# Gate and up products in two halves, with their low sums in banks of the other group

## The chip, the cores and the metric

The kernel runs on one core of a Trainium2 chip. The metric is the time of one execution in device microseconds; before the change the median of 3 runs is 1695.89 us (1694.25 to 1705.35).

## The reference

Two request groups, 256 prompt frames and 64 new frames of a running stream, go through one layer with shared weights. Together they are T = 320 columns of D = 2048 features. The part that the change touches is the feed-forward network behind the second norm:

```
hn = rmsnorm(h, norm_ffn[l])
gu = hn @ w_gate_up[l]                                   # 2048 -> 2 x 5632
h = h + (silu(gu[..., :D_FF]) * gu[..., D_FF:]) @ w_down[l]
```

Ahead of it stand the norm, the input projection, stick-breaking attention, the spatial gate, the two branch projections and w_out; behind it the last norm. All data is float32.

## The kernel before, in words

Features lie on the 128 partitions, the 320 columns along the free dimension. Every float32 product is made of three products of shorter floats: a weight chunk `raw` is loaded on SP's queue, ACT rounds it to `wh` (line 554 in the feed-forward part, line 70 elsewhere) and DVE takes the rest, `wl` or `low` (lines 555 and 71). Three `raw` buffers and four `wh` buffers stand in a ring: the load of a chunk waits until DVE has split the chunk three before it, and a cast to `wh` waits until PE is through with the chunk four before it.

The feed-forward part runs in three slices of 16, 16 and 12 blocks of 128 hidden features. A slice takes four blocks at a time, as a *gate quad* and then an *up quad* (`quad`), so 8, 8 and 6 quads, and then multiplies by w_down: first six blocks side by side in two passes over k, then one block after the other (lines 87 to 89).

One quad works on four blocks and all 16 row chunks of 128, which come as 8 loads of 512 KB. For each load PE runs 20 *wide* products (line 562; two row chunks times five column pieces, with a piece of the activations as the stationary operand and 512 weight columns moving), in three main banks: three `acc` banks for a gate quad, three of four `aux` banks for an up quad. They give the sum with frames on partitions. After all 8 loads the 64 *low* products follow (line 572): four sums of 16, one per block, in the banks `aux1`, `aux`, `aux1`, `aux`, that DVE copies to `total` (line 573). A quad's low products need the low parts of all 8 chunks, so these stay until the last of the four sums; there are nine buffers for them.

The main banks have to be turned: `quad_turn` has ACT copy the three banks into `flat`, once for each 16-bit half (line 587, three copies each), and issue a DMA transpose after each three (line 588). `quad_join` has DVE put the transposed halves back (line 594, two), and add them to `total` (lines 596, 597). Then a gate quad's total is scaled and goes through Silu (lines 601, 602); an up quad's is scaled, multiplied with the gate's and split into `act` (lines 606 to 611).

Each engine runs its instructions in a fixed order, which a planner makes from the order in the code. Work that is late by intent is put off by ticks: `at(now + 5, ...)` calls a function when five ticks have gone by; a tick ends with each loaded chunk and, before the change, with each low sum.

In the w_out loop ahead of it, POOL's queue loads the residual input x in tiles `xr` (line 524), the first two as soon as the norm's result is there.

Of the kernel before, what the change touches and what calls it, by code (L numbers as in the profile page):

```python
# [34 lines left out]
def stream_step(ctx: ExitStack, tc: tile.TileContext, xT, w_in, w_a, w_b, w_out, w_gu, w_down,  # L35
# [484 lines left out]
    for m in range(KD):  # L520
        x = t320("xr")
# [18 lines left out]
    count = [0]  # L540

    def quad(b0, main, done):
        lows = []
        for c in range(0, KD, 2):
            raw = wraw.tile([P, HALF * P], F32, tag="raw", name="raw")
            nc.sync.dma_start(out=raw.rearrange("p (b k) -> p b k", b=4),
                              in_=w_gu[b0 : b0 + 4, :, c * P : (c + 2) * P].rearrange("b p k -> p b k"))
            wh = wsplit.tile([P, HALF * P], F32R, tag="wh", name="wh")
            if count[0] % 9 < 4:
                wl = wsplit.tile([P, HALF * P], F32R, tag="wl", name="wl")  # L550
            else:
                wl = fpool.tile([P, HALF * P], F32R, tag="low", bufs=5, name="low")
            count[0] += 1
            nc.scalar.copy(out=wh, in_=raw)  # L554
            nc.vector.tensor_tensor(out=wl, in0=raw, in1=wh.bitcast(F32), op=ALU.subtract)  # L555
            wh = wh.rearrange("p (b k) -> p b k", b=4)
            lows.append(wl)
            for j in range(2):
                k = c + j
                w, x = wh[:, :, j * P : (j + 1) * P], hg[k][2]  # L560
                for i, at0 in enumerate((0, T + TS, P, T + TS + P, TP)):
                    nc.tensor.matmul(main[i // 2].rearrange("p (b m) -> p b m", b=4), x[:, at0 : at0 + P], w,  # L562
                                     start=k == 0 and i % 2 == 0, stop=k == KD - 1 and (i % 2 == 1 or i == 4))
            tick()
        total = fpool.tile([P, 4, T], F32, tag="sum", bufs=2, name="sum")
        now = state["tick"]
        turning = quad_turn(main)
        for b in range(4):
            ps = aux1() if b % 2 == 0 else aux()
            for k in range(KD):  # L570
                at0 = (2 * b + k % 2) * P
                nc.tensor.matmul(ps[:, :T], lows[k // 2][:, at0 : at0 + P], hg[k][0], start=k == 0, stop=k == KD - 1)  # L572
            nc.vector.tensor_copy(total[:, b, :], ps[:, :T])  # L573
            tick()
# [16 lines left out]
    def quad_join(total, flat, turned):  # L591
# [12 lines left out]
    def up_out(gate, total, b):  # L604
# [3 lines left out]
        for j in range(2):  # L608
            a = pair("act", dt=F32R)
            nc.scalar.copy(out=a[:, 0, :], in_=t[:, j, :])  # L610
            nc.vector.tensor_tensor(out=a[:, 1, :], in0=t[:, j, :], in1=a[:, 0, :].bitcast(F32), op=ALU.subtract)
            act.append(a)
# [57 lines left out]
    def down_out(m, ps):  # L670
        nc.vector.tensor_tensor(out=hs[m], in0=ps[:, :T], in1=hs[m], op=ALU.add)
        if s0 + n < KF:
            return
# [6 lines left out]

    for s0, n in SLICES:
        act = []
        for b0 in range(s0, s0 + n, 4):
            gate = quad(b0, [acc() for _ in range(3)], gate_out)
            quad(KF + b0, [aux() for _ in range(3)], lambda total, b, gate=gate: up_out(gate, total, b))
        final = s0 + n == KF
        lead = [acc() for _ in range(3)] + [aux() for _ in range(3)]
        for k0, k1 in ((0, HALF), (HALF, n)):
            for m, ps in enumerate(lead):
# [3 lines left out]
                if k1 == n:  # L693
                    down_out(m, ps)
                tick()
        halves = [(t[:, 0, :], t[:, 1, :]) for t in act]
        for m in range(len(lead), KD - LATE if final else KD):
            down_out(m, block(w_down[m][:, s0 * P : (s0 + n) * P], halves))
# [147 lines left out]
```

## Time and profile before

| | us |
|---|---|
| median of 3 runs | 1695.89 (1694.25 to 1705.35) |
| the profiled execution | 1698.68 |
| its span | 1696.9 |
| PE busy | 1682.7 |
| DVE busy | 971.8 |
| ACT busy | 734.1 |

PE is the engine that multiplies; PEld are its weight loads, which overlap the products. Busy times of PE are modelled, so the pace of PE is read from when its instructions start, not from how long one lasts. The granted clock is 0.998 of full speed over the whole span. The span is what lies between the first and the last instruction, and the execution takes 1.8 us more.

### The profile page before, as it was taken

What the parts mean: (1) busy time and instruction counts of PE and PEld (TensorE: products, weight loads), DVE (VectorE), ACT (ScalarE), POOL (GpSimd) and SP (SyncE); (2) the same over time, 40 slices, a digit from 0 to 9 for tenths busy, and PEclk for the clock granted to TensorE, in tenths of its full rate; (3) what the DMA queues carried; (4) which work ended last, traced back from release to release, by engine and by line L of the source; (5) the groups of instructions that cost most, each with busy time, mean ns of one, the idle gap of its engine ahead of it and who ended that gap; (6) DMA issues with size and microseconds to landing.
All of it is one profiled execution on the core that took longest, in us unless ns stands there. A gap on an engine that the chain in (4) does not pass through costs nothing.

```text
span 1696.9 us, 25604 instructions
## 1 busy us (share of the span) xinstructions
PE 1682.7 (99%) x10496; PEld 1607.0 (95%) x10496; DVE 971.8 (57%) x1261; ACT 734.1 (43%) x956; POOL 38.9 (2%) x68
## 2 busy tenths in 40 slices
PE   9999999999999999999999999999999999999998
PEld 9999999999999999998988899988888999889898
DVE  7665656544444445556666664446666644475666
ACT  7555645433333333444444532343445323444343
POOL 1100001000000000000000000000000000000000
PEclk9999999999999999999999999999999999999999
DMA  7866555444444444556656655566666545566554
GB/s 280 258 178 177 160 163 164 118 152 151 151 149 149 150 149 162 173 167 178 175 173 182 193 167 150 156 166 170 180 167 189 166 150 162 164 189 174 149 156 124
DMA packets 236982, 285.49 MB, mean 168 GB/s; under 512 B 98081, under 2 KB 194337, under 8 KB 236865
## 3 DMA queue, kind: packets, MB, share of 16 engines
q1 hardware_dynamic: 164016, 257.72, 48.6%
q10 hardware_dynamic: 70224, 17.88, 6.0%
q0 software_dynamic: 2624, 8.26, 1.6%
q8 instruction: 82, 1.34, 0.3%
q14 instruction: 36, 0.29, 0.1%
HBM read 256.03 MB, written 5.51 MB: 154 GB/s over the span
## 4 chain that ended last, share of the span: by engine, by line
PE 87%; DMA 5%; DVE 4%; ACT 2%; issue 1%; ACTq 0%; SPq 0%; DVEq 0%
PE acc L89 18%; PE acc L87 18%; PE acc L88 18%; PE acc L562 9%; PE aux L572 8%; PE aux L562 7%; DMA raw<-w_gu 2%; DMA turned<-flat 2%; PE aux L89 2%; PE aux L88 2%; PE aux L87 2%; ACT flat L587 1%; DVE low L555 1%; DVE flat L594 1%; PE acc L639 1%
## 5 line engine op out<-in xcount | busy, mean ns | idle before, releaser
L70 ACT CAST wh<-raw 128x1024 fp32r<-128x1024 f32 (+2 forms) x296 | 302.7, 1023 | 561.1 <-PE acc L88 382.4
L71 DVE TENSOR_TENSOR wl<-raw,wh 128x1024 fp32r<-128x1024 f32 (+2 forms) x296 | 351.7, 1191 | 224.4 <-ACT wh L70 223.3
L87 PE MATMUL acc<-A,wh 128*128 128x320 f32 x1088 | 337.7, 311 | 0.4 <-ACT A L108 0.4
L88 PE MATMUL acc<-A,wh 128*128 128x320 f32 x1088 | 336.5, 309 | 0.0
L89 PE MATMUL acc<-A,wl 128*128 128x320 f32 x1088 | 336.3, 309 | 0.0
L554 ACT CAST wh<-raw 128x1024 fp32r<-128x1024 f32 x176 | 185.3, 1054 | 317.8 <-DMA raw<-w_gu 259.9
L87 PEld LDWEIGHTS acc<-A,wh 128*128 128x128 f32 x1088 | 204.4, 188 | 2.3 <-issue 1.5
L88 PEld LDWEIGHTS acc<-A,wh 128*128 128x128 f32 x1088 | 204.5, 188 | 0.3 <-DVE A L110 0.3
L89 PEld LDWEIGHTS acc<-A,wl 128*128 128x128 f32 x1088 | 204.3, 188 | 0.2 <-DVE wl L71 0.2
L562 PE MATMUL acc<-wh,A 128*128 128x512 f32 x880 | 203.2, 390 | 1.1 <-ACT wh L554 1.0
L562 PE MATMUL aux<-wh,A 128*128 128x512 f32 x880 | 201.5, 389 | 0.0
L562 PEld LDWEIGHTS acc<-wh,A 128*128 128x128 f32 x880 | 164.2, 188 | 37.0 <-ACT wh L554 3.5
L562 PEld LDWEIGHTS aux<-wh,A 128*128 128x128 f32 x880 | 164.8, 188 | 33.7
L89 PE MATMUL acc<-act,wl 128*128 128x320 f32 x500 | 155.1, 311 | 2.8 <-DVE wl L71 2.8
L87 PE MATMUL acc<-act,wh 128*128 128x320 f32 x500 | 155.0, 310 | 0.0
L88 PE MATMUL acc<-act,wh 128*128 128x320 f32 x500 | 154.9, 310 | 0.0
L555 DVE TENSOR_TENSOR low<-raw,wh 128x1024 fp32r<-128x1024 f32 x96 | 117.8, 1235 | 37.4 <-ACT wh L554 37.1
L573 DVE COPY sum<-aux 128x320 f32<-128x320 f32 x88 | 43.0, 489 | 157.8 <-PE aux L572 157.8
L572 PE MATMUL aux<-A,low 128*128 128x320 f32 x768 | 128.6, 309 | 0.1
L572 PEld LDWEIGHTS aux<-A,low 128*128 128x128 f32 x768 | 117.1, 188 | 1.4 <-ACT flat L587 0.4
L555 DVE TENSOR_TENSOR wl<-raw,wh 128x1024 fp32r<-128x1024 f32 x80 | 97.6, 1224 | 22.1 <-ACT wh L554 22.1
L572 PE MATMUL aux<-A,wl 128*128 128x320 f32 x640 | 109.0, 309 | 0.8 <-ACT flat L587 0.8
(221 smaller groups left out, 2297.5 us busy)
## 6 DMA issues: line engine op xcount, KB each, us to landing
raw<-w_gu SPq DMA_DIRECT2D x176, 512.0 KB, 3.8
raw<-w_in SPq DMA_DIRECT2D x141, 512.0 KB, 3.7
raw<-w_down SPq DMA_DIRECT2D x80, 512.0 KB, 3.7
raw<-w_out SPq DMA_DIRECT2D x32, 512.0 KB, 3.6
raw<-w_a SPq DMA_DIRECT2D x16, 512.0 KB, 3.4
raw<-w_b SPq DMA_DIRECT2D x16, 512.0 KB, 3.5
raw<-w_down SPq DMA_DIRECT2D x16, 256.0 KB, 2.8
xr<-xT POOLq DMA_DIRECT2D x16, 160.0 KB, 2.6
```

The lines of the kernel that those rows point to most:

```text
L70: nc.scalar.copy(out=wh[:, : n * P], in_=raw[:, : n * P])
L71: nc.vector.tensor_tensor(out=wl[:, : n * P], in0=raw[:, : n * P], in1=wh[:, : n * P].bitcast(F32), op=ALU.subtract)
L87: nc.tensor.matmul(ps[:, :T], a, x[0], start=first, stop=False)
L88: nc.tensor.matmul(ps[:, :T], a, x[1], start=False, stop=False)
L89: nc.tensor.matmul(ps[:, :T], b, x[0], start=False, stop=last)
L554: nc.scalar.copy(out=wh, in_=raw)
L555: nc.vector.tensor_tensor(out=wl, in0=raw, in1=wh.bitcast(F32), op=ALU.subtract)
L562: nc.tensor.matmul(main[i // 2].rearrange("p (b m) -> p b m", b=4), x[:, at0 : at0 + P], w, start=k == 0 and i % 2 == 0, stop=k == KD - 1 ...
L572: nc.tensor.matmul(ps[:, :T], lows[k // 2][:, at0 : at0 + P], hg[k][0], start=k == 0, stop=k == KD - 1)
L573: nc.vector.tensor_copy(total[:, b, :], ps[:, :T])
L587: tc.keep_in_program_order(nc.scalar.copy(out=planes[:, i, c * 512 : (c + 1) * 512], in_=hw[:, :, 1 - i]))
L594: nc.vector.tensor_copy(rows[:, :, :, :, 1 - i], turned[:, i].rearrange("p (c b) t -> p b c t", c=3))
```

## The change

`quad` goes through the row chunks in two halves: 4 loads with 40 wide products, then four low sums over these 4 chunks, then the same again. The wide products stay in the three main banks for both halves. The first half's low sums are copied to `total`, those of the second half are added to it. They take banks of either group: `BESIDE` lists them for a gate quad (turn 0) and an up quad (turn 1), half by half. The low parts have two sets of four buffers in turn. `total` has three buffers in place of two, and `quad_join` stands behind the last add in the planner's order. The put-off work counts from the end of the low sums: the join comes 3 ticks later, the output work 4 and 5; two low sums make one tick. The loads of x use the tag `ev`, which the gates use before them. `up_out` and `down_out` get arguments that leave their work as it is in the calls made here; `add_down` and the tag of `gate_quad` are not used.

```diff
-        x = t320("xr")
+        x = t320("ev")
...
+    LOWS = 4
+    MAIN = (acc, aux)
+    BESIDE = (((aux,) * 4, (aux, aux, aux1, aux)), ((acc, acc, acc, aux1), (acc, acc, aux, aux1)))
+
+    def quad(src, xs, done, tag="sum"):
...
+        main = [MAIN[turn_no]() for _ in range(3)]
+        total = fpool.tile([P, 4, T], F32, tag=tag, bufs=3 if tag == "sum" else 1, name=tag)
+        for half, c0 in enumerate((0, nk // 2)):
+            lows = []
+            for c in range(c0, c0 + nk // 2, 2):
...
+                if count[0] % (4 + LOWS) < 4:
+                    wl = wsplit.tile([P, HALF * P], F32R, tag="wl", name="wl")
+                else:
+                    wl = fpool.tile([P, HALF * P], F32R, tag="low", bufs=LOWS, name="low")
...
+            if half:
+                turning = quad_turn(main)
+            for b in range(4):
+                ps = BESIDE[turn_no][half][b]()
+                for k in range(nk // 2):
...
+                if half:
+                    last = nc.vector.tensor_tensor(out=total[:, b, :], in0=ps[:, :T], in1=total[:, b, :], op=ALU.add)
+                else:
+                    nc.vector.tensor_copy(total[:, b, :], ps[:, :T])
+                if b % 2:
+                    tick()
         now = state["tick"]
-        turning = quad_turn(main)
-        for b in range(4):
-            ps = aux1() if b % 2 == 0 else aux()
...
-        at(now + 5, quad_join, total, *turning)
+        at(now + 3, quad_join, last.ins, total, *turning)
         for i in range(2):
-            at(now + 6 + i, done, total, 2 * i)
+            at(now + 4 + i, done, total, 2 * i)
...
-    def quad_join(total, flat, turned):
+    def quad_join(behind, total, flat, turned):
+        with tc.issue_after(behind):
+            join(total, flat, turned)
```

How this moves instructions is seen at three places. The names are those of the tiles, `aux` with a number is the single bank `aux1`, and xN is a run of N alike. The first is PE's order over one gate quad. Before, in slice one:

```order
L562 MATMUL acc<-wh,A 128x512 x80
L572 MATMUL aux_7831<-A,wl 128x320 x8
L572 MATMUL aux_7831<-A,low 128x320 x8
L572 MATMUL aux<-A,wl 128x320 x8
L572 MATMUL aux<-A,low 128x320 x8
L572 MATMUL aux_7867<-A,wl 128x320 x8
L572 MATMUL aux_7867<-A,low 128x320 x8
L572 MATMUL aux<-A,wl 128x320 x8
L572 MATMUL aux<-A,low 128x320 x8
```

With the change, a gate quad (`acc`) and the first half of the up quad behind it (`aux`):

```order
L571 MATMUL acc<-wh,A 128x512 x40
L580 MATMUL aux<-A,wl 128x320 x32
L571 MATMUL acc<-wh,A 128x512 x40
L580 MATMUL aux<-A,low 128x320 x16
L580 MATMUL aux_8363<-A,low 128x320 x8
L580 MATMUL aux<-A,low 128x320 x8
L571 MATMUL aux<-wh,A 128x512 x40
L580 MATMUL acc<-A,wl 128x320 x24
```

The 80 wide products in a row are now 40 and 40, and half of the low products stand between them. A sum is 8 products long in place of 16, and the up quad's sums lie in `acc`.

The second place is DVE's order from the join of an up quad through the gate quad behind it. Before (an up quad's join, and the splits of the next gate quad):

```order
L594 COPY flat<-turned 128x1536
L573 COPY sum<-aux 128x320
L594 COPY flat<-turned 128x1536
L555 TENSOR_TENSOR low<-raw,wh 128x1024
L596 TENSOR_TENSOR sum<-flat,sum 128x1280
L555 TENSOR_TENSOR low<-raw,wh 128x1024
L597 TENSOR_TENSOR sum<-flat,sum 128x4x64
L555 TENSOR_TENSOR wl<-raw,wh 128x1024
L606 TENSOR_TENSOR sum<-sum,rh 128x640 x2
L607 TENSOR_TENSOR sum<-sum 128x640 x2
L555 TENSOR_TENSOR wl<-raw,wh 128x1024
L611 TENSOR_TENSOR act<-sum,act 128x320 x4
```

With the change, from the join to the last split of the gate quad's second half:

```order
L612 COPY flat<-turned 128x1536 x2
L564 TENSOR_TENSOR low<-raw,wh 128x1024
L614 TENSOR_TENSOR sum<-flat,sum 128x1280
L564 TENSOR_TENSOR low<-raw,wh 128x1024
L615 TENSOR_TENSOR sum<-flat,sum 128x4x64
L564 TENSOR_TENSOR low<-raw,wh 128x1024
L624 TENSOR_TENSOR sum<-sum,rh 128x640
L585 COPY sum<-aux 128x320
L625 TENSOR_TENSOR sum<-sum 128x640
L585 COPY sum<-aux 128x320
L624 TENSOR_TENSOR sum<-sum,rh 128x640
L631 TENSOR_TENSOR act<-sum,act 128x320 x2
```

and what follows these at once:

```order
L625 TENSOR_TENSOR sum<-sum 128x640
L585 COPY sum<-aux 128x320 x2
L631 TENSOR_TENSOR act<-sum,act 128x320 x2
L564 TENSOR_TENSOR low<-raw,wh 128x1024
L564 TENSOR_TENSOR wl<-raw,wh 128x1024 x3
L583 TENSOR_TENSOR sum<-aux,sum 128x320
L564 TENSOR_TENSOR wl<-raw,wh 128x1024
L583 TENSOR_TENSOR sum<-aux,sum 128x320
L583 TENSOR_TENSOR sum<-aux_9307,sum 128x320
L583 TENSOR_TENSOR sum<-aux,sum 128x320
```

The join of line 612 (594 before) waits for both transposes and stands behind all four sums of its quad, where it stood ahead of the last one. The splits of lines 564 that follow it are those of the second half of the quad that PE is in, the three of the row `x3` and the one behind the next add belong to the first half of the quad after that. The adds of line 583 are mixed with these.

The third place is ACT's order round the turn of that same gate quad with the change:

```order
L628 CAST act<-sum 128x320 x4
L563 CAST wh<-raw 128x1024 x3
L601 COPY flat<-acc 128x512 x3
L563 CAST wh<-raw 128x1024
L602 DMA_TRANSPOSE turned<-flat 128x12x128
L601 COPY flat<-acc 128x512 x3
L602 DMA_TRANSPOSE turned<-flat 128x12x128
L563 CAST wh<-raw 128x1024 x4
```

The casts `x3` ahead of the copies of line 601 are the first three chunks of the next quad. The copies stood behind three such casts before, too.

## Rows read from the trace of the kernel before

**Rows 1.** The page: span; busy time, share and count of each engine.
```profile
span 1696.9 us, 25604 instructions
...
PE 1682.7 (99%) x10496; PEld 1607.0 (95%) x10496; DVE 971.8 (57%) x1261; ACT 734.1 (43%) x956; POOL 38.9 (2%) x68
```

**Rows 2.** Stretches: length, busy of PE, PEld, DVE, ACT, POOL; clock; DMA.
```profile
760.88:981.19 220.31, 220.31 (x1154) 195.19 (x1153) 137.05 (x162) 105.27 (x138) 2.15 (x1) 1.00 0.65 179
1093.84:1318.34 224.50, 222.49 (x1154) 194.71 (x1153) 133.74 (x155) 101.78 (x133) 0.00 (x0) 1.00 0.64 174
1431.65:1596.90 165.25, 165.25 (x866) 146.41 (x865) 95.06 (x111) 75.00 (x98) 0.00 (x0) 1.00 0.62 175
1600.40:1603.70 3.30, 3.30 (x14) 3.30 (x15) 3.30 (x4) 0.00 (x0) 0.00 (x0) 0.56 0.61 169
```

**Rows 3.** Chain of waits, one quad: start, length, work.
```profile
871.20 18.16 PE acc L562 x80
889.36 9.38 PE aux L572 x64
```

**Rows 4.** Timeline of PE at the last slice's down blocks.
```profile
1596.90 0.31 PE L87 MATMUL acc<-act,wh 128*128 128x320 f32 x1
...
1600.33 0.64 PE L89 MATMUL acc<-act,wl 128*128 128x320 f32 x1 [2.39 <-DVE wl L71]
...
1603.38 0.30 PE L88 MATMUL acc<-act,wh 128*128 128x320 f32 x1
```

**Rows 5.** Waits of PE: us in total, times, longest.
```profile
PE acc L89 <- DVE wl L71: 2.8, 2, 2.4
```

**Rows 6.** Timeline of all engines in slice two, round a stall.
```profile
1208.43 1.07 DVE L594 COPY flat<-turned 128x1536 uint16<-128x1536 uint16 x1 [4.58 <-DMA turned<-flat]
...
1210.70 1.22 DVE L555 TENSOR_TENSOR low<-raw,wh 128x1024 fp32r<-128x1024 f32 x1
...
1215.45 1.05 ACT L554 CAST wh<-raw 128x1024 fp32r<-128x1024 f32 x1 [5.59 <-DMA raw<-w_gu]
...
1216.55 0.73 PE L562 MATMUL acc<-wh,A 128*128 128x512 f32 x2 [0.61 <-ACT wh L554]
```

**Rows 7.** Timeline of all engines, one quad's turn.
```profile
1227.35 1.55 ACT L587 COPY flat<-acc 128x512 uint16<-128x512 uint16 x3
...
1232.17 1.45 ACTq L588 DMA_TRANSPOSE turned<-flat  x1
...
1237.29 1.07 DVE L594 COPY flat<-turned 128x1536 uint16<-128x1536 uint16 x1 [2.56 <-DMA turned<-flat]
```

**Rows 8.** Transposes of the turned tile, all of them.
```profile
DMA to landing us min/median/max: 3.6/3.7/6.1
```

**Rows 9.** Groups: busy us, mean ns | idle, releaser.
```profile
L554 ACT CAST wh<-raw 128x1024 fp32r<-128x1024 f32 x176 | 185.3, 1054 | 317.8 <-DMA raw<-w_gu 259.9 <-PE acc L88 28.0 <-PE acc L562 22.5
...
L555 DVE TENSOR_TENSOR low<-raw,wh 128x1024 fp32r<-128x1024 f32 x96 | 117.8, 1235 | 37.4 <-ACT wh L554 37.1 <-PE aux L572 0.2
...
L594 DVE COPY flat<-turned 128x1536 uint16<-128x1536 uint16 x44 | 45.3, 1051 | 40.6 <-DMA turned<-flat 40.6
L573 DVE COPY sum<-aux 128x320 f32<-128x320 f32 x88 | 43.0, 489 | 157.8 <-PE aux L572 157.8
...
L596 DVE TENSOR_TENSOR sum<-flat,sum 128x1280 f32<-128x1280 f32 x22 | 32.8, 1492 | 0.0
...
L611 DVE TENSOR_TENSOR act<-sum,act 128x320 fp32r<-128x320 f32 x44 | 18.7, 491 | 0.1
...
L607 DVE TENSOR_TENSOR sum<-sum 128x640 f32<-128x640 f32 x22 | 17.1, 822 | 0.0
...
L671 DVE TENSOR_TENSOR h<-acc,h 128x320 f32<-128x320 f32 x33 | 16.2, 491 | 35.5 <-PE acc L89 35.5
...
L597 DVE TENSOR_TENSOR sum<-flat,sum 128x256 f32<-128x256 f32 x22 | 9.4, 426 | 0.0
```

**Rows 10.** Loads of line 524.
```profile
DMA to landing us min/median/max: 2.5/2.6/4.5
```

More of the change, by code (lines that the diff above doesn't have):

```diff
@@ L539, in stream_step @@
     fpool = fctx.enter_context(tc.tile_pool(name="ffn", bufs=1))
[L540 to L565, printed above, removed]
-        now = state["tick"]
-        turning = quad_turn(main)
-        for b in range(4):
-            ps = aux1() if b % 2 == 0 else aux()
[L570 to L574, printed above, removed]
-        at(now + 5, quad_join, total, *turning)
@@ L602, in gate_out, with up_out @@
         nc.scalar.activation(out=t, in_=t, func=AF.Silu)
-    def up_out(gate, total, b):
+    def up_out(to, apart, gate, total, b):
         t = total[:, b : b + 2, :]
@@ L610, in up_out, with add_down @@
             nc.scalar.copy(out=a[:, 0, :], in_=t[:, j, :])
-            nc.vector.tensor_tensor(out=a[:, 1, :], in0=t[:, j, :], in1=a[:, 0, :].bitcast(F32), op=ALU.subtract)
-            act.append(a)
+            flat = a.rearrange("p i t -> p (i t)")
+            for r0, r1, at0 in (((TP, T, T), (0, TP, T + TS)) if apart else ((0, T, T),)):
+                nc.vector.tensor_tensor(out=flat[:, at0 : at0 + r1 - r0], in0=t[:, j, r0:r1],
+                                        in1=a[:, 0, r0:r1].bitcast(F32), op=ALU.subtract)
+            to.append(a)
+    def add_down(m0, total, b):
+        y = ypair[(m0 + b) // 2]
+        nc.vector.tensor_tensor(out=y, in0=total[:, b : b + 2, :], in1=y, op=ALU.add)
     def gain(m, half):
@@ L668, in stream_step, with down_out @@
     LATE = 6
-    def down_out(m, ps):
+    def down_out(m, ps, final):
         nc.vector.tensor_tensor(out=hs[m], in0=ps[:, :T], in1=hs[m], op=ALU.add)
-        if s0 + n < KF:
+        if not final:
             return
@@ L679, in down_out, with gate_quad, up_quad @@
         nc.vector.tensor_scalar(out=hs[m], in0=hs[m], scalar1=g_fin[:, m : m + 1], scalar2=None, op0=ALU.mult)
+    wide_x = [t[2] for t in hg]
+    def gate_quad(b0, tag="sum"):
+        return quad(w_gu[b0 : b0 + 4], wide_x, gate_out, tag)
+    def up_quad(b0, gate, to, apart):
+        quad(w_gu[KF + b0 : KF + b0 + 4], wide_x, lambda total, b: up_out(to, apart, gate, total, b))
     for s0, n in SLICES:
@@ L683, in stream_step @@
         for b0 in range(s0, s0 + n, 4):
-            gate = quad(b0, [acc() for _ in range(3)], gate_out)
-            quad(KF + b0, [aux() for _ in range(3)], lambda total, b, gate=gate: up_out(gate, total, b))
+            up_quad(b0, gate_quad(b0), act, False)
         final = s0 + n == KF
```

28 lines of the change are left out of this document (26 added, 2 removed).

## The prediction

> **What bounds the kernel now.** I read the page first: PE is busy for 1682.7 of 1696.9 us, and no other engine for more than 58% [rows 1]. So all the time in which PE waits, from the first instruction to the last, is 14.2 us, 0.84% of the span. The change takes no product away (a quad keeps 80 wide and 64 low ones), so its gain has a ceiling below 1%.
>
> Next the chain of waits in an undisturbed stretch, for PE's pace: 80 wide products in 18.16 us (0.227 each), 64 low ones in 9.38 us (0.147 each), 27.54 us a quad [rows 3]. The last low product is followed by the next quad's first wide one with no gap; changing kind or bank costs nothing that the view shows.
>
> Then the stretches, one for the quads of each slice [rows 2]. The first has 8 quads in 220.31 us, which is 8 x 27.54; the third 6 in 165.25, which is 6 x 27.54. Only the second is longer: 224.50, so 4.19 us of stalls. Round one of them [rows 6] the reader sees how it comes about: DVE sits 4.58 us in the join at line 594 for a transpose, and the split of a chunk stands behind the join in its queue; that split ends at 1211.92, its raw buffer is loaded again and the cast begins at 1215.45, 3.53 us later; PE starts its wide products at 1216.55, having waited.
>
> The other place is the start of the down blocks. In the last slice 17 products start from 1596.90 up to 1603.38, 6.48 us where 17 x 0.147 are 2.49: 3.99 us lost, of which 2.39 are a wait for DVE's split [rows 4]. The rest is the clock: it is granted at 0.56 on average over the 3.3 us behind the wait [rows 2], so part of them ran at 1.2 GHz. The same wait in an earlier slice cost the other 0.4 of 2.8 us [rows 5].
>
> What the change can give back is therefore 4.19 + 3.99 + 0.4 = **8.6 us**.
>
> **The change, part by part.**
>
> *Halves.* No product more or less, and switches between wide and low cost nothing by rows 3. What changes is cover. Before, the nine buffers of low parts held a whole quad of eight chunks until its last low sum, so DVE could split only one chunk ahead. Now a half holds four of eight buffers, and DVE splits the next half's four while PE is in this one (the order shows the splits of the second half ahead of the copies of the first half's sums). A load has then 13.77 us of PE's time to come for every four chunks; one takes 3.53 from split to cast [rows 6]. The 4.19 us go. At the down blocks the first four splits now stand ahead of the join, so the 4.4 us there go too.
>
> *Sums.* 88 copies become 88 copies and 88 adds on DVE. The copy takes 0.489 us, an add out of PSUM into SBUF of the same size 0.491 (line 671) [rows 9]: 43 us more on an engine that is idle for 725. Beside PE's work this is nothing; what it does to DVE's queue is the next point.
>
> *DVE's queue behind the join.* This is the price. Put 0 at the end of an up quad's last wide product, with a gate quad next. ACT copies the main banks at once; from the first copy to the second transpose's issue it is 4.82 us [rows 7]; the transpose lands after 3.7 at the median [rows 8]. DVE joins from 8.5 on. Then, in the order of the new rows, and with the mean durations [rows 9]: two joins 2.1, a split 1.24, 1.49 for line 596, a split, 0.43 for line 597, a split: 16.3. Four scalings at 0.82, four subtractions for act at 0.49, four copies at 0.49 and the fourth split: 24.7. PE needs that split for its low sums at 27.54, so this is just in time.
>
> But the raw buffer of the third chunk of the next quad comes free only then. Its cast begins 3.53 later, at 28.3, and ends at 29.3 [rows 6, 9]. ACT's copies of the gate quad's main banks, ready at 27.54, stand behind that cast. The fourth cast follows the first three copies (1.55 us, [rows 7]) and ends at 31.9, its split at 33.2, and DVE's add of the second low sum, which stands behind the split, at 33.7. That sum lies in the third main bank of the up quad to come. PE has ended the gate quad's low products at 27.54 + 4.69 = 32.23, and reaches this bank with its fifth wide product, 0.91 later, at 33.1. **It waits 0.6 us.**
>
> There is one such place for each gate quad behind an up quad of its slice, and PE waits at the up quad that follows: 3 + 3 + 2 = 8 places, 4.6 us. Behind a gate quad's join DVE has 1.64 us to do in place of 5.2, and by the same count the fourth split ends 3.6 us earlier: no wait. Ends of the range: below, 0 a place, since instructions of DVE that follow each other overlap a little (the 44 of line 611 would be 21.6 us by their mean and are 18.7 [rows 9], 0.07 each), which over the 17 on this path is more than 0.6. Above, the longest landing, 6.1 us [rows 8], shifts everything by 2.4: 3.0 a place, 24 us. I take 0.6, with the median landing: the long ones come where several loads are issued next to the transpose, and here DVE has no more than one split to do between its adds and the join.
>
> *Join and output later.* The join is issued 2 chunks later and behind the last add. Its own transposes keep their place on ACT's queue. Who waits: the single `flat` tile, needed again 27 us on; and `act` at the slice's end, needed in the second pass of the down blocks, 21 us (six blocks of 24 products at 0.147) behind the last low sum. By the queue above it is ready some 20 us behind the last wide product, 15 behind the last low sum. Nothing.
>
> *x in `ev`.* POOL's loads of x wait for the last gates, no longer for the first norm; the two early ones move behind all other loads of POOL's queue. They land in 2.6 us, 4.5 at most [rows 10]; between the last gate and the first add of x lie the branch products and w_out's first block, 96 products of 0.147, 14 us. Nothing; without that cover 2.6 us once. The buffers for `total`, and the new arguments, issue no instruction.
>
> **The sum.** 1698.7 (the profiled execution) - 8.6 + 4.6 = 1694.7. That execution is 2.8 above the median of the runs, so **1692 us** against 1695.9, less than can be told from no change (about 1%, 17 us).
>
> **The rivals.**
>
> *The backlog of DVE's queue is deeper.* From 1.1 us a place on (8.6 / 8) the change gives back more than it takes, which is a join only 0.5 us later than I count. The trace has such joins: one began 5.1 us after the issue [rows 7], 1.4 later than the median landing, so 2.0 a place, 16 us, and 1703. With the longest landing 24 us: 1711. For it speaks that the wait closes on itself: late splits make late loads, these make late copies, these a late join. Against it that a gate quad's join is lighter and resets the queue. Slower by over 1% needs 3.2 us a place, more than the longest landing gives alone; a load that is late too could do it.
>
> *It doesn't do what it says.* Three slices with the same order have 0, 4.19 and 0 us of stalls in the quads, so these hang on when transposes land, and the join still stands ahead of a split. If the new cover does not reach, the stalls stay: 1696.
>
> *Half the clock.* PE's clock fell to its lower level behind a wait of 2.4 us [rows 2, 4]. If bank changes, now every 8 low products, left such holes, the low parts would run at that level: 11 products took 3.05 us there, 0.277 each [rows 4], so 64 x 22 x 0.13 = 183 us more, 1875. The trace speaks against it: banks change every 16 low products now, and the clock stays at 1.00 through all quads [rows 2]. By that row the low parts add 0. The Trainium skill has the rule that speaks for this rival (TensorE: Matmul & The Clock Gate, "A second HAM failure mode: psum-queue depth-cycling"): going through PSUM banks in each iteration can leave PE short idle times between its groups, frequent enough for the clock to swing between its levels and cost throughput. By it the sum would be 1875 in place of 1692.
>
> **How the numbers follow.** My forecast (waits under 1.1 us a place): 0.60, from 1687 to 1696. The backlog: 0.30, 1696 to 1711, of which 0.05 slower by over 1%. No effect: 0.07. The clock: 0.03. Slower by over 1% is then 0.08, faster by over 1% 0.01 (the ceiling forbids it; the rest is for what I have not seen), no change 0.91. The range for 8 in 10 runs from 1685 (all 8.6 back, and the runs' spread of 1.6 downward) to 1705 (2.0 us a place, and 1.6 upward); it leaves out the upper half of the backlog and the clock.
>
> **What would show it.** In the second slice eight quads in 220.3 us plus three waits; no wait of line 89 for a split at the last down blocks, and the clock at 1.00 there. Each up quad but a slice's first begins with four wide products and then a wait of about 0.6 us that DVE's add (line 583) ends. The first copy of line 601 comes 1 to 2 us behind the last wide product of these gate quads, at once in up quads. I am wrong if PE waits anywhere else in the quads, if these waits are over 1.1 us, or if the low products are further apart than 0.147 us.

## The result, and the profile after

Over 20 runs of each, the changed kernel takes **1706.55 us** at the median (1700.59 to 1711.09), the kernel before 1697.11 (1691.75 to 1708.54): ratio 1.0047, 95% interval 1.0032 to 1.0062. It is half a per cent slower, 9.4 us. The profiled executions are 12.4 us of span apart; the places below add up to that. The one of the changed kernel, at 1711.09, is the slowest of its 20, so it shows more waiting than a median run: 1706.55 is 16 us above the 1690.4 of runs below that have no waits in the quads, and the trace has 20.2.

The page of the changed kernel, the lines that answer to [rows 1]:

```profile
span 1709.3 us, 25850 instructions
...
PE 1687.4 (99%) x10496; PEld 1607.4 (94%) x10496; DVE 1007.5 (59%) x1349; ACT 736.0 (43%) x956; POOL 39.3 (2%) x68
```

The quads of its three slices, as in [rows 2] (length; busy time of PE, PEld, DVE, ACT, POOL; clock; DMA), then 4.4 us behind its longest wait, and the start of the last down blocks:

```profile
761.01:991.15 230.14, 224.63 (x1154) 196.43 (x1153) 152.25 (x196) 105.47 (x138) 2.15 (x1) 0.99 0.65 174
1103.79:1329.91 226.12, 221.66 (x1154) 194.85 (x1153) 148.36 (x189) 102.37 (x133) 0.00 (x0) 1.00 0.64 176
1442.55:1612.87 170.32, 167.63 (x866) 147.31 (x865) 110.09 (x139) 76.55 (x98) 0.00 (x0) 0.99 0.65 175
...
962.16:966.60 4.44, 4.43 (x11) 3.51 (x12) 0.74 (x2) 1.48 (x2) 0.00 (x0) 0.50 1.18 278
...
1612.87:1640.00 27.13, 27.13 (x187) 27.13 (x186) 16.98 (x27) 10.70 (x19) 0.00 (x0) 1.00 0.42 112
```

All three slices are now longer than their products need, by 20.2 us together (the floor is 220.5, 220.5 and 165.4, as runs below show). The last row has PE busy throughout and the clock at 1.00: the stall of [rows 4] is gone.

Next come DVE's wait at the join and PE's waits in the quads (us in total, times, longest), then the group of the join (before: [rows 9], line 594), then the transfers (queue, count, KB where given, and at the end the median us from issue to landing):

```profile
DVE flat L612 <- DMA turned<-flat: 88.0, 18, 7.0
PE aux L571 <- DVE sum L583: 11.9, 8, 3.2
PE acc L571 <- DVE sum L583: 0.6, 1, 0.6
```

```profile
L612 DVE COPY flat<-turned 128x1536 uint16<-128x1536 uint16 x44 | 43.7, 1050 | 112.5 <-DMA turned<-flat 88.0 <-ACT wh L563 20.5 <-ACT wh L70 4.0
```

```profile
raw<-w_gu SPq DMA_DIRECT2D x176, 512.0 KB, 4.0
...
turned<-flat ACTq DMA_TRANSPOSE x44, 5.3
```

PE waits where the prediction said, at an up quad's wide products for DVE's add, and hardly elsewhere (11.9 of 12.5 us). At the first such place of slice two it is the very sign that the prediction gave, four wide products and then a short wait:

```profile
1186.49 1.09 PE L571 MATMUL aux<-wh,A 128*128 128x512 f32 x4
1187.74 2.57 PE L571 MATMUL aux<-wh,A 128*128 128x512 f32 x10 [0.16 <-DVE sum L583]
```

The two starts are 1.25 us apart where four products need 0.91, so 0.3 us are lost. But the waits grow along a slice. DVE stands idle ahead of the join's first copy for 112.5 us in place of 40.6 [rows 9], 5.1 a quad, and the transposes land after 5.3 us in place of 3.7 [rows 8].

The timeline of all engines round the longest wait shows how one hangs on the other (start, length, engine, line; in brackets the idle time before it):

```profile
929.27 2.40 ACTq L602 DMA_TRANSPOSE turned<-flat  x1
...
937.55 1.99 DVE L612 COPY flat<-turned 128x1536 uint16<-128x1536 uint16 x2 [7.99 <-ACT wh L563]
939.43 1.21 DVE L564 TENSOR_TENSOR low<-raw,wh 128x1024 fp32r<-128x1024 f32 x1
...
943.43 1.21 DVE L564 TENSOR_TENSOR low<-raw,wh 128x1024 fp32r<-128x1024 f32 x1
...
949.95 2.00 ACT L563 CAST wh<-raw 128x1024 fp32r<-128x1024 f32 x2
950.71 1.22 DVE L564 TENSOR_TENSOR low<-raw,wh 128x1024 fp32r<-128x1024 f32 x1
...
955.90 0.63 PE L571 MATMUL aux<-wh,A 128*128 128x512 f32 x2
957.00 1.04 ACT L563 CAST wh<-raw 128x1024 fp32r<-128x1024 f32 x1 [5.05 <-DMA raw<-w_gu]
957.95 1.55 ACT L601 COPY flat<-acc 128x512 uint16<-128x512 uint16 x3
958.08 1.23 DVE L564 TENSOR_TENSOR wl<-raw,wh 128x1024 fp32r<-128x1024 f32 x1 [3.88 <-ACT wh L563]
959.22 0.48 DVE L583 TENSOR_TENSOR sum<-aux,sum 128x320 f32<-128x320 f32 x1
959.76 0.93 PE L571 MATMUL aux<-wh,A 128*128 128x512 f32 x2 [3.23 <-DVE sum L583]
...
961.63 1.28 DVE L583 TENSOR_TENSOR sum<-aux,sum 128x320 f32<-128x320 f32 x3
```

The second transpose is issued at 929.27. It lands 8.2 us later, at 937.4, and that ends DVE's 7.99 us (the bracket names a cast that ended at about the same time; the join doesn't read it). Of the three splits behind the join, 939.43 to 944.64, two have had their casts since 933.8. The last split of that quad comes at 950.71, so the next quad's raw loads are late, its cast at 957.00 has waited 5.05 us for one, and the flat copies at 957.95, which ACT could have begun at 950.9 when the wide products ended, stand behind that cast. So the next transposes are late too. DVE's add at 959.22 stands behind the split that this cast feeds; PE waits for it, then again for the next adds. Behind those waits PE runs at a clock of 0.50 (1.2 GHz): the wide products are 0.427 us apart instead of 0.227.

The circle tightens along a slice: the flat copies of its gate quads begin 0.5 us before, then 1.0, 1.5 and 7.1 us behind the end of their wide products in slice one, -0.5, 1.0, 2.0 and 5.0 in slice two, and -0.5, 0.9 and 3.8 in slice three.

### The profile page after: what moved, and what is told of

Read it like the earlier page. It is cut to its first block, busy times and chain, and to the rows that moved or that the text cites. A ratio compares the mean times of both kernels' runs of the same rounds, so it can differ in the third digit from the quotient of the medians.

```text
span 1709.3 us, 25850 instructions
## 1 busy us (share of the span) xinstructions
PE 1687.4 (99%) x10496; PEld 1607.4 (94%) x10496; DVE 1007.5 (59%) x1349; ACT 736.0 (43%) x956; POOL 39.3 (2%) x68
## 4 chain that ended last, share of the span: by engine, by line
PE 80%; DVE 7%; DMA 6%; issue 3%; ACT 3%; ACTq 1%; SPq 0%; DVEq 0%
PE acc L87 18%; PE acc L88 18%; PE acc L89 18%; PE aux L571 9%; PE acc L571 3%; DMA raw<-w_gu 3%; PE aux L580 3%; DMA turned<-flat 3%; PE acc L580 2%; PE aux L89 2%; PE aux L88 2%; PE aux L87 2%; ACT flat L601 1%; DVE low L564 1%; ACT wh L563 1%
## 5 line engine op out<-in xcount | busy, mean ns | idle before, releaser
L89 PE MATMUL acc<-A,wl 128*128 128x320 f32 x1088 | 336.3, 309 | 0.0
L571 PE MATMUL aux<-wh,A 128*128 128x512 f32 x880 | 210.6, 397 | 12.1 <-DVE sum L583 11.9
L89 PEld LDWEIGHTS acc<-A,wl 128*128 128x128 f32 x1088 | 204.2, 188 | 0.6 <-DVE wl L71 0.5
L564 DVE TENSOR_TENSOR wl<-raw,wh 128x1024 fp32r<-128x1024 f32 x88 | 107.0, 1224 | 86.0 <-ACT wh L563 86.0
L89 PE MATMUL acc<-act,wl 128*128 128x320 f32 x500 | 154.5, 309 | 0.0
L564 DVE TENSOR_TENSOR low<-raw,wh 128x1024 fp32r<-128x1024 f32 x88 | 108.5, 1233 | 9.8 <-ACT wh L563 9.8
L612 DVE COPY flat<-turned 128x1536 uint16<-128x1536 uint16 x44 | 43.7, 1050 | 112.5 <-DMA turned<-flat 88.0
L87 PEld LDWEIGHTS acc<-act,wh 128*128 128x128 f32 x500 | 93.9, 188 | 0.0
L89 PEld LDWEIGHTS acc<-act,wl 128*128 128x128 f32 x500 | 93.9, 188 | 0.0
L88 PEld LDWEIGHTS acc<-act,wh 128*128 128x128 f32 x500 | 93.9, 188 | 0.0
```

The lines of the kernel that those rows point to most:

```text
L87: nc.tensor.matmul(ps[:, :T], a, x[0], start=first, stop=False)
L88: nc.tensor.matmul(ps[:, :T], a, x[1], start=False, stop=False)
L89: nc.tensor.matmul(ps[:, :T], b, x[0], start=False, stop=last)
L612: nc.vector.tensor_copy(rows[:, :, :, :, 1 - i], turned[:, i].rearrange("p (c b) t -> p b c t", c=3))
```

## The experiments

Each is the changed kernel with one edit, but for before_late, which is the kernel before. "Lost" is what the quads of all slices take over the 606.4 us that many runs below reach; "standstill" is DVE's idle time at the join's first copy, by 22 quads; in brackets stands the time of copies put there instead. Both are from the profiled execution, the median is over all runs. Each kernel ran on one chip beside the kernel before, and its ratio is to that.

| run | what | median us | lost | standstill a quad |
|---|---|---|---|---|
| changed | | 1706.55 | 20.2 | 5.1 |
| late6 | join behind the 6th split | 1690.42 | 0 | 0.5 |
| late5 | join behind the 5th split | 1690.54 | 0 | 1.0 |
| nowait | join reads nothing of the transposes | 1690.68 | 0 | 0 |
| halfload | half the bytes of each load | 1690.56 | 0 | 3.4 |
| halfturn | half of each transpose | 1690.41 | 0 | 0.3 |
| adds_first | 4th split behind the adds | 1702.14 | 13.9 | 5.1 |
| flatfirst | that, and two casts behind flat copies | 1690.85 | 0 | 3.4 |
| cut62 | chunks cut 6 and 2 | 1690.43 | 0 | 0.3 |
| cut62_pin | that, join held ahead of the 5th split | 1709.48 | 20.4 | 5.9 |
| hold7 | no wait, DVE held 3.5 us by copies | 1690.69 | 0 | (3.5) |
| hold13 | the same, 6.4 us | 1713.58 | 21.5 | (6.4) |
| hold13_late6 | 6.4 us behind the 6th split | 1708.69 | 19.8 | (6.4) |
| extra_pin | adds_first, one more half transpose | 1700.93 | 8.9 | 1.9 |
| extra_late6 | late6, one more half transpose | 1691.1 | 0 | 0.4 |
| cut26 | chunks cut 2 and 6 | 1714.19 | 4.7 | 2.1 |
| before_late | kernel before, join two splits later | 1692.35 | -0.5 | 0.2 |

**Is it the join's place in DVE's queue? (late6, late5)** The join is called five (four) ticks later and queued behind the newest split; a slice's last up quad stays as it was.

```
-        at(now + 3, quad_join, last.ins, total, *turning)
+        at(now + 3 + wait, quad_join, last.ins, total, *turning)     # wait = 5 (late5: 4)
...
-        with tc.issue_after(behind):
+        with tc.issue_after(state["split"].ins):
```

> Changed kernel with one edit: on DVE the join (two copies from the transposed planes) stands behind the sixth split of the next quad instead of right behind the last add, with its outputs as much later; the last up quad of a slice as it was. Theory 'held queue': in the changed kernel DVE stands 88 us in all in the join's first copy, waiting for the transposes, and the next quad's splits behind it, its raw loads, casts and flat copies go late from quad to quad. Then DVE's wait at the join falls from 88 us to under 40, PE's 12 us of waits for the add go to under 2, the 20 us by which the quads are over their floor go to under 4, and the time goes from 1706.5 to 1687 to 1692. Rival 'too much on DVE' (the 43 us of adds, whatever the order): DVE's busy time is the same, the waits stay, 1702 to 1709.

Ratio 0.9961 [0.9942, 0.998]. The quads in this run, and the group of the join:

```profile
761.16:981.64 220.48, 220.48 (x1155) 195.14 (x1153) 153.95 (x196) 105.64 (x138) 2.15 (x1) 1.00 0.68 181
1094.28:1314.78 220.50, 220.50 (x1155) 195.15 (x1154) 150.44 (x189) 102.09 (x133) 0.00 (x0) 1.00 0.68 181
1427.42:1592.80 165.38, 165.38 (x867) 146.36 (x866) 111.22 (x139) 76.09 (x99) 0.00 (x0) 1.00 0.68 180
```

```profile
L613 DVE COPY flat<-turned 128x1536 uint16<-128x1536 uint16 x44 | 43.5, 1048 | 12.1 <-DMA turned<-flat 12.1
```

PE is busy for the whole of each stretch. One turn of it, timeline of ACT's queue and DVE:

```profile
899.33 1.85 ACTq L603 DMA_TRANSPOSE turned<-flat  x1
...
902.53 1.23 DVE L564 TENSOR_TENSOR low<-raw,wh 128x1024 fp32r<-128x1024 f32 x1 [2.89 <-ACT wh L563]
...
904.80 1.23 DVE L564 TENSOR_TENSOR low<-raw,wh 128x1024 fp32r<-128x1024 f32 x1 [1.04 <-ACT wh L563]
905.94 1.97 DVE L613 COPY flat<-turned 128x1536 uint16<-128x1536 uint16 x2
```

Two splits run while the transpose is on its way, and the join begins 6.6 us behind its issue without a wait, though the transposes land no sooner than in the changed kernel (median 5.7). DVE does no less: 18.9 us of work a quad, against 18.7. So the 43 us of adds are no bound, as predicted. With the waits the spread of the runs is gone too: 1690.02 to 1691.26, against 1700.59 to 1711.09 for the changed kernel and 1691.75 to 1708.54 for the kernel before.

> Changed kernel with the join one split later on DVE (behind the fifth split of the next quad, where behind the sixth gave 1690.4 and behind the fourth, the changed kernel, 1706.5), its outputs one chunk later. If what stands behind the join costs by what the wait has left, most of the 16 us go with one split (it takes 1.2 us of DVE itself, and lets one more raw load start ahead of the wait): DVE's wait at the join 30 to 60 us in place of 88, quads within 4 us of their floor, 1689 to 1694. If it needs the sixth (the chunk whose load is late is the seventh or later): 1696 to 1703.

Ratio 0.9943 [0.9926, 0.9959]: one split is enough.

**Is the wait for the transposes all of it? (nowait)** Join and sums work on the sum tile alone.

```
-            nc.vector.tensor_copy(rows[:, :, :, :, 1 - i], turned[:, i]...)
+            nc.vector.tensor_copy(spare, total.bitcast(U16)...[:, 1280 * i : 1280 * (i + 1)])
...
-        nc.vector.tensor_tensor(out=total, in0=rows[:, :, 0:T], in1=total, op=ALU.add)
+        nc.vector.tensor_tensor(out=total, in0=total, in1=total, op=ALU.add)
```

> Changed kernel in which the join reads nothing of the transposed planes (its two copies and two sums of the same kind work on the sum tile alone; the transposes still run and nobody reads them, so the planes are left out of the result). DVE's instructions, the order of PE and ACT, the transposes and the loads stay. 'Held queue': the only thing taken away is DVE's wait for the landing, so PE's waits for the add go to 0 to 1 us, the flat copies begin with the end of the wide products in every quad, 1686 to 1691. 'Too much on DVE': as before the edit, 1702 to 1709. If the banks alone made the waits (adds late behind PE, not behind DVE): also 1702 to 1709.

Ratio 0.9961 [0.9944, 0.9977]. All of the loss goes with that wait, with the banks and the adds as they were. (Two things moved beside it. The copies of this size take 0.49 us instead of 1.05, so 1.1 us a quad of work went too; the hold runs below put more than that back. And the fifth split now stands behind the join's two sums, not ahead of them, which holds it longer, not shorter.)

**Why do the transposes land later? (halfload, halfturn)** In the kernel before, raw loads were in flight at the issue of 8 of the 44 transposes; in the changed kernel at all 44.

```
-                nc.sync.dma_start(out=raw..., in_=src[:, :, c * P : (c + 2) * P]...)
+                nc.sync.dma_start(out=part, in_=src[:, :, c * P : (c + 1) * P]...)   # read twice by cast and split
```

```
-            nc.scalar.dma_start_transpose(out=turned[:, i], in_=planes[:, i, :])
+            nc.scalar.dma_start_transpose(out=turned[:, i], in_=planes[:, i, 0 : 6 * P])   # read twice by the join
```

> Changed kernel in which each raw load of the quads brings half the bytes (256 KB; cast and split read each half block twice, so every second block of the weights is left out of the result). Theory 'loads beside the transposes': in the kernel before no load was in flight beside most transposes and they landed in 3.65 to 3.7 us; in the changed kernel one to three are and the median is 5.3. With half the bytes the landings go to 3.7 to 4.5 median, DVE's wait at the join from 88 to 45 to 65 us, PE's waits for the add to under 2, the time to 1687 to 1693. Rival 'the landing has another cause' (the place of the transposes in their queue, DVE's or ACT's use of memory): the landings stay over 5.0; the loads alone land sooner, 1692 to 1703.

```profile
raw<-w_gu SPq DMA_DIRECT2D x176, 256.0 KB, 2.7
...
turned<-flat ACTq DMA_TRANSPOSE x44, 4.1
```

```profile
L614 DVE COPY flat<-turned 128x1536 uint16<-128x1536 uint16 x44 | 43.8, 1051 | 73.8 <-DMA turned<-flat 68.0 <-ACT wh L565 5.8
```

Ratio 0.997 [0.9953, 0.9986]. The same transposes land 1.2 us sooner when only the loads' bytes are halved. Part of that could come from the waits that went with it, but nowait loses nothing either, keeps its 512 KB, and its transposes land after 4.9; so some 0.8 us of it is the loads' doing. DVE still stands 3.4 us a quad, a little more than I had expected, and that costs nothing.

> Changed kernel in which each of the two transposes turns half of its plane (the other half of the result's planes is a copy of the first, so half of the planes is left out); the raw loads keep their 512 KB, the join's copies their size and their place behind the adds (the fourth split falls behind the third add instead of the first, which by itself gave 4 us). It parts the landing from the loads, which the run with half loads shortened together. Theory 'a join ahead of the splits costs what the landing lasts': landings median 3.0 to 4.2 us in place of 5.3, DVE's wait at the join 40 to 65 us in place of 88, raw loads still 3.5 or more, quads within 3 us of their floor, 1688 to 1693. Rival 'it was the loads' own length that the half loads took away': the backlog stays, 1697 to 1704.

Ratio 0.9957 [0.9938, 0.9976]; loads keep their 512 KB (median 3.5), transposes land after 4.4, the standstill is 5.6 us in all, smaller than I expected since the second transpose is also issued sooner (3.0 us behind the wide products, not 5.4).

**Is it the split between the adds? (adds_first)**

```
-                nc.vector.tensor_tensor(out=wl, in0=raw, in1=wh.bitcast(F32), op=ALU.subtract)
+                sub = lambda: nc.vector.tensor_tensor(out=wl, in0=raw, in1=wh.bitcast(F32), op=ALU.subtract)
+                if c == 6 and state.get("last"):      # the last add of the quad before
+                    with tc.issue_after(state["last"]):
+                        sub()
```

> Changed kernel with one edit: the fourth split of the next quad stands behind the four adds on DVE, where it stood between the first and the second. Theory 'split between the adds' (the prediction's link: the add that frees the third main bank stands behind a split that waits for a late load): PE's 12 us of waits for the add go to under 1, and if that is all that the backlog costs, the time goes to 1688 to 1693. 'Held queue': the join still holds DVE, DVE's wait there stays over 70 us, loads and casts go on being late, and what PE no longer waits at the banks it waits at wide or low products; 1695 to 1704.

```profile
DVE flat L618 <- DMA turned<-flat: 97.7, 20, 7.2
...
PE aux L576 <- DVE sum L588: 7.0, 4, 3.3
```

Ratio 1.0039 [1.0021, 1.0057]: only a third of the loss goes, as "held queue" had it. The link I had priced was real and not the main cause.

**Does the loss grow through ACT's queue? (flatfirst)** The same, with ACT's third and fourth cast of the next quad behind the first and the last three flat copies, and the fifth split held behind the join. (The third split falls behind the first add by this.)

```
+                if c in (4, 6) and ("flat", c // 2 - 2) in state:
+                    with tc.issue_after(state["flat", c // 2 - 2]):      # flat copy 3, 6
+                        nc.scalar.copy(out=wh, in_=raw)
```

> The order with the four adds first (1702.1), and on ScalarE the third cast of the next quad behind the first three flat copies and the fourth behind the last three, with the fifth split held behind the join as it was. If the loss grows from quad to quad because flat copies, and with them the transposes and the next join, stand behind a cast whose load is late, this breaks the circle: flat copies begin with the end of the wide products everywhere, DVE's wait at the join 4 to 5 us in every quad, lost time from 14 us to 0 to 5, 1690 to 1696. If the circle runs through raw loads and splits alone: 1699 to 1704.

```profile
L627 DVE COPY flat<-turned 128x1536 uint16<-128x1536 uint16 x44 | 43.8, 1051 | 75.4 <-DMA turned<-flat 75.4
```

Ratio 0.9951 [0.993, 0.9973]. The flat copies begin with the end of the wide products in every quad, and the standstill stays under the changed kernel's though the transposes land no sooner (4.7 at the median). The circle is broken at another link.

**What does a standstill of known length cost? (hold7, hold13, hold13_late6)** nowait with 7 or 13 more copies of 0.49 us, and the next split queued behind them; the join is called one tick later (five in hold13_late6).

```
+        for _ in range(7):     # 13
+            held = nc.vector.tensor_copy(spare, total.bitcast(U16)...)
```

> The changed kernel with the join that waits for no transfer (1690.7), and seven more copies of 0.49 us at its place between the fourth and the fifth split: DVE is held there for 4.4 us by its own work, where the changed kernel's two copies and their wait hold it for 7.2 us on average. 'The standstill's length is the price': something between, quads' lost time 0 to 6 us, 1690 to 1697. If every hold ahead of the fifth split costs: 1698 or more.

> The same with thirteen copies: held for 7.3 us at that place, as long as the changed kernel on average, with no transfer waited for (the four copies of the first sums stand among them, and two splits behind the adds). 'The standstill's length is the price, whatever causes it': the quads lose 10 to 40 us again, 1700 to 1730. If it is the transfers (loads beside transposes) and not DVE's queue: 1690 to 1694.

> The same thirteen copies and the join behind the sixth split, the seventh held behind them. 'It is what stands behind the standstill': two raw loads more are under way before DVE is held, the quads stay within 5 us of the floor: 1690 to 1696. If DVE's total of work is the bound: as with thirteen at the other place, within 4 us of it.

Ratios 0.9942 [0.9918, 0.9966], 1.0099 [1.0069, 1.013] and 1.0057 [1.0033, 1.008]. Held by 3.5 us of copies, PE loses nothing; by 6.4 it loses 21.5 us, with no transfer waited for. PE takes 27.56 us a quad. With seven copies DVE's work in it is 21.1 us (463.5 by 22), more than the 18.7 of the changed kernel, and nothing is lost: the amount of work on DVE is not what makes the changed kernel slow. With thirteen it is some 25 us (24.8 in the trace, over four quads in the middle of slice one), and the third run is a miss: I held that only what stands *behind* the standstill counts, but the same copies behind the sixth split lose 19.8 us, as I had written for the case that DVE's total of work is the bound. So the two runs with thirteen copies don't part a standstill from too much work. What is shown is that the price is not in proportion: a standstill of 3.4 us a quad costs nothing (halfload), one of 5.1 costs 20.2 us. Where between them it sets in, no run tells. late6 does not move the standstill, it removes it, because the transfer lands while DVE splits.

**Does the time to the next quad decide? (cut62, cut62_pin, cut26)** The row chunks parted otherwise.

```
-        for half, c0 in enumerate((0, nk // 2)):
+        for half, (c0, c1) in enumerate(((0, 12), (12, nk))):     # cut26: 4
```

> Changed kernel with the row chunks parted 6 and 2: the low products behind the wide ones last 2.4 us, the next quad begins 2.4 us sooner after the transposes' issue. 'A join ahead of the splits': DVE's wait at the join grows by 1 to 2 us a quad or its backlog shows on PE, PE's waits in the quads grow from 20 us to 30 to 60, 1715 to 1750. Rival 'the four and four cut was bad for another reason (banks, adds)': no order by the cut, within 5 us of 1706.

Ratio 0.9958 [0.994, 0.9977], the opposite of what I expected, and for a reason that makes the run another one: the instruction order shows the join behind the *sixth* split here, since the first half's six splits now come earlier. It is late6 by another way. So I held the fifth split behind the join:

```
+                if c == 8 and state.get("joined"):      # the join's second copy
+                    with tc.issue_after(state["joined"].ins):
+                        sub()
```

> The 6 and 2 cut again, with the fifth split of the next quad held behind the join by an edge, since without that edge the join had fallen behind the sixth split there by itself. Now the join stands where the changed kernel has it, and the next quad begins 2.4 us sooner after the transposes' issue. 'A join ahead of the splits': DVE's wait at the join over 70 us and PE's lost time in the quads 20 to 60 us: 1705 to 1750. If the cut itself helps (only two chunks' sums left behind the wide products): 1690 to 1696.

```profile
DVE flat L617 <- DMA turned<-flat: 123.5, 21, 8.9
```

Ratio 1.0064 [1.0046, 1.0083]. At the old place the loss is back, 20.4 us, at the low end of what I had given. It is no more than the changed kernel's, though the next quad begins 2.4 us sooner: the place of the join decides, and a price of that time itself is not shown.

> Changed kernel with the row chunks of a quad parted 2 and 6 in place of 4 and 4: the low products behind the wide ones last 7.1 us in place of 4.7, so the next quad begins 2.4 us later after the transposes' issue. 'A join ahead of the splits costs what is left of the landing': DVE's wait at the join falls by about 2 us a quad, from 88 to 45 to 60 us, quads within 4 us of the floor, 1688 to 1694. 'Too many sums on DVE' or 'banks': adds, copies and banks are the same, 1700 to 1707.

Median 1714.19 of four runs between 1701 and 1730, ratio 1.0135 [1.0085, 1.0184]: not what I expected, and not explained. The profiled execution is the fastest of the four (1701.01), with 4.7 us lost in the quads, at a standstill of 2.1 us, and 4.8 us of PE's waits for splits at the down blocks; the slower three have no trace. Six of the eight tiles of low parts are then held until the last low sum, which may be the cause; no run tells.

**The later join without the halves (before_late).** The same edit on the kernel before.

```
-        at(now + 5, quad_join, total, *turning)
+        at(now + 5 + wait, quad_join, total, *turning)     # wait = 4, join behind the newest split
```

> Kernel before (low sums whole, nothing of the change) with the one edit that mended the changed kernel: the join stands behind two more splits of the next quad, its outputs as much later, the last up quad of a slice as it was. If the place of the join is all there was to gain, the quads come to their floor of 220.3, 220.3 and 165.3 us here too, 4.2 us less than before, and the last down blocks keep their waits of 4 us: 1690.5 to 1693.5, and the halves bring 1 to 3 us beside it. If the halves are needed for it, the quads of the second slice keep their 4 us: 1694 to 1697.

```profile
761.52:981.84 220.32, 220.32 (x1154) 195.20 (x1153) 136.46 (x163) 105.90 (x138) 2.15 (x1) 1.00 0.65 179
1094.48:1314.81 220.33, 220.33 (x1155) 195.20 (x1153) 132.85 (x156) 101.94 (x133) 0.00 (x0) 1.00 0.66 179
1427.45:1592.71 165.26, 165.26 (x867) 146.40 (x865) 95.80 (x112) 75.13 (x98) 0.00 (x0) 1.00 0.63 175
```

Ratio 0.9975 [0.9958, 0.9991]. The 4.2 us of slice two go without the halves; these bring 1.9 us more (1690.43 of cut62, on the same chip at the same time, against 1692.35).

**Longer landing, on purpose (extra_pin, extra_late6).** One more transpose of half a plane, read by nobody, meant to stand ahead of the second one. In ACT's order of both traces it stands ahead of the first one, in all 22 quads.

```
+            if i:
+                more = fpool.tile([P, 6, P], U16, tag="more", name="more")
+                nc.scalar.dma_start_transpose(out=more, in_=planes[:, 0, 0 : 6 * P])
```

> The order of the run with the four adds first (1702.1; join behind the fourth split), held by an edge, with one more transpose of half a plane issued ahead of the second one into a tile that nobody reads, so that the second lands some 2 to 3 us later after the first. 'A join ahead of the splits costs what the landing lasts': DVE's wait at the join over 110 us in place of 113, and the quads' lost time from 14 us to 30 to 70: 1718 to 1760. Rival 'a backlog that saturates, or is not the landing's': 1698 to 1706.

> The same extra half transpose in the kernel with the join behind the sixth split (1690.4). If the join behind the sixth split takes the landing off the path, 2 to 3 us more of it find the room that is there: 1690 to 1693. If the landing had been mended by chance (close to the edge): 1700 or more.

Waits in extra_pin:

```profile
ACT flat L610 <- issue: 94.9, 22, 6.4
DVE flat L624 <- DMA turned<-flat: 41.0, 22, 3.3
```

The first (ratio 1.0007 [0.9979, 1.0034]) is a miss, and no test of a longer landing: ACT stood up to 6.4 us a quad in issuing the two transposes that now follow each other, so the casts came later, fewer loads lay beside the last transpose (median 3.7, issued 9.2 us behind the wide products instead of 6.4), and DVE's standstill fell to 41 us. PE lost 8.9 us. The second (ratio 0.9946 [0.9928, 0.9964]) shows that late6 has some room: the last transpose lands 11.5 us behind the wide products at the median, not 10.0, and the quads lose nothing.

## Why the prediction was wrong

The sum of the spans, by places: the old stalls of slice two -4.2; the floor of the quads +0.5 (606.4 against the 605.9 of before_late); new waits +20.2; the down blocks -4.2 (-0.66 in slice two's, -3.54 in the last); the start +0.1: 12.4 us. Predicted were -8.6 and +4.6.

*What the change gives back* was right at the down blocks, -4.2 for -4.4: the L89 waits of [rows 5] are gone, and the clock is 1.00 at the last ones. The -4.2 of slice two is only bookkeeping. In the changed kernel that slice is still 5.6 us over its floor (226.12 against 220.50), and its waits begin where the old ones did, with DVE in the join and splits behind it; only the last link is another, DVE's add in place of ACT's cast. So the cover that the halves were to bring did not reach. before_late ends the old stalls without the halves.

*That switches cost nothing* was nearly right: 0.02 us a quad, 0.5 in all.

*The new wait* was right in kind and place, and wrong in size: 20.2 us for 4.6. The step that failed is the one that chose its row: "I take 0.6, with the median landing: the long ones come where several loads are issued next to the transpose, and here DVE has no more than one split to do between its adds and the join." The median of [rows 8] is that of transposes with little beside them: 36 of 44 have no load in flight at their issue, and 36 meet at most one until they land (3.7 at the median). The eight that meet two or three took 4.9, and over slice two from 1160 to 1320, where the old stalls are, the median is 5.1; so the row was there. In the changed kernel PE goes on to the next quad 4.7 us behind the wide products instead of 9.4, so loads are in flight at the issue of all 44, 32 meet two or three, and the median is 5.3. halfload shows the cause by taking half of the bytes away: 4.1 and nothing lost. With 5.3 in place of 3.7 the prediction's own sum gives 2.2 us a place and 17.6 in all, near the 20.2 of the trace. That is luck in part, for the places are not alike: the first ones of the slices lose 0.3 us or nothing, the late ones microseconds. The Trainium skill has the rule (DMA: Bandwidth & Descriptors, "Queues, rings and completion order"): a DMA engine with work on several queue rows takes a packet of each in turn. These landings agree with it: 3.7 us at the median for the 18 transposes before that ran with no load in flight at all, up to 8.2 beside loads.

*"A gate quad's join is lighter and resets the queue"* was wrong too. DVE's standstill is 4 to 8 us behind gate and up quads alike, and what is carried on is not only DVE's backlog but ACT's: flat copies behind a late cast make the next transposes late. flatfirst cuts that link and loses nothing. So eight waits of 0.6 became a few late in each slice, the longest 3.2 us.

*The price of a wait* left out the clock: behind the waits of slices one and three PE runs some 20 wide products at 0.427 instead of 0.227 us, about 4 of the 20.2 us. The prediction had this cost for the old stall [rows 4] and did not put it on the new one.

*The rivals.* The deeper backlog (0.30, 1696 to 1711) is what happened, by the loop that it named, "the wait closes on itself". What I set against it was the reset. The range ended at 1705, short of the 1711 that it gave for the longest landing at every place. *It doesn't do what it says* (0.07, 1696) had the mechanism too, that the join still stands ahead of a split, but the stalls grew where it had them stay. Half the clock did not come: late6, whose banks change as often, has the clock at 1.00 and PE busy throughout all quads, so the Trainium skill's rule on depth-cycling (TensorE: Matmul & The Clock Gate, "A second HAM failure mode: psum-queue depth-cycling") took nothing here; what the clock took came behind the waits for DVE's adds. *Sums, x in `ev`, outputs later* cost nothing, as said: late6 has all three and no wait.

## What to carry to other kernels

When a change moves transfers together in time, a landing time from the old trace is the wrong row unless the same neighbours were in flight there: take the landings of those that met as many, however few (here 4.9 us of eight, not 3.7 of all). Look in each in-order queue for an instruction that waits on a transfer, count the independent work behind it, and put as much of it ahead as the landing lasts; here one split ahead of the join was worth 16 us. **late6** (and late5, cut62, flatfirst) beats both kernels: 1690.42 us, 0.4% under the kernel before.

## What the runs showed of the hardware

A transpose of 128 x 1536 two-byte values from SBUF to SBUF landed in 3.7 us (median of 18 in the kernel before, 5.0 at most) with no load in flight, and in 3.8 to 8.2 in the changed kernel, always beside loads of 512 KB. A standstill of DVE of 3.4 us a quad cost PE nothing (halfload) and one of 5.1 cost 20.2 us. Two transposes issued one behind the other kept ACT from its next copy for up to 6.4 us (extra_pin, 94.9 us in 22 times).
